# The last four gate tiles of a recurrent stage made as two wide seven-product pairs

## The chip, the cores and the metric

The kernel runs on one core of one Trainium2 chip. The metric is the time of one execution on the device in microseconds (us), as the median of several runs. The core's engines are TensorE (PE, matmuls), VectorE (DVE), ScalarE (ACT), GpSimd (POOL) and SyncE (SP); here POOL and SP mostly issue DMAs, SP the weights.

## The reference

One decoder layer on 512 tokens of width 1024, all in float32: a SwiGLU product, a gated merge of attention and a linear recurrence, and a second SwiGLU product, each with norms around it. The part at hand is the merge:

```python
proj = u @ w_in[l]
q, k, v, xr, yr, gl = jnp.split(proj, splits, axis=-1)
...
attn_d = attn.astype(x.dtype).reshape(B, S, ATTN_OUT_WIDTH) @ w_attn_branch[l]
rec = rg_lru_branch(xr, conv_w[l], conv_b[l], lru_w_x[l], lru_b_x[l],
                    lru_w_a[l], lru_b_a[l], lru_a_param[l]) * jax.nn.gelu(yr)
rec_d = rec @ w_rec_branch[l]
gates = jax.nn.sigmoid(gl).reshape(B, S, N_BRANCHES, D_MODEL)
merged = gates[:, :, 0] * attn_d + gates[:, :, 1] * rec_d
h = h + rms_norm(merged @ w_out[l], mix_norm_post[l])
```

`rg_lru_branch` is a causal convolution over four tokens (`xr` to `xc`), two gates of `xc` (sigmoids of products with block-diagonal weights, four heads of 256), and the scan h = a·h + b along the tokens.

## The kernel before, in words

Activations lie transposed: 128 of the 1024 features on the partitions, the 512 tokens along the row. So a result of width 1024 is eight tiles of 128x512, and a product over 1024 features has eight chunks of 128.

*Three-product form.* PE multiplies in the format fp32r, and the kernel keeps float32's accuracy by splitting each operand in a high and a low part (`split`, L303 and L304: ACT writes the high part, DVE subtracts it for the low part). `mm3` adds high·high, high·low and low·high (L316 to L318). A plain tile is 8 chunks x 3 = 24 matmuls of 128x512. Its weights (128x1024) come by one DMA on SP's queue into one of four raw buffers and go through one split into one of four buffers `w8`.

*Seven-product form.* Two neighbouring tiles and the two halves of the tokens make a 2x2 product by blocks, which Strassen's scheme (in Winograd's form) does in seven products instead of eight. The sums of the input (`um_t` for the plain halves and the "forms" p4 to p7) are made once, ahead of the stage. The sums of the weights are made for each pair by `w_forms_within`: two raw buffers, four additions of 512 (L725 to L729), and splits of 512, 1024, 1024 and 1024. `seven_wide` then issues the products, each as 4 matmuls of 512 (L791) and 4 of 256 (L794); between them ACT moves a partial sum from one accumulator to the next (L799, `move`), and `fold` (L805 on ACT, L807 or L809 on DVE) and `sum_of` (L815, L817, L819) bring the two halves of a bank together.

*The stage.* `LRU_ORDER` lists the steps: the branch that goes through gelu (`branch`, four pairs already in seven-product form), the convolution input (`conv`, plain tiles with taps at L1610), the recurrence's gates and scan (`gates`, `gates_of` and `recur`: L1669 to L1698), and the gate gl's second half for the merge (`gate1`: plain tiles, copied by L1651 to `sig`, sigmoid at L1644). Before, gate tiles 0 and 1 follow conv 2, tiles 2, 3, 4 follow conv 3, and tiles 5, 6, 7 follow gates 3. Behind the loop come the products with w_rec: tiles 0 to 2 at once (chunks 0 to 5, then 6, then 7), then tiles 3 to 7; L1741 multiplies each by the gate, L1742 adds the gated attention output (`facc`), L304 splits the sum.

Each engine runs its instructions in one fixed order. The framework's scheduler sets it when the program is built: by the order of the code, priorities (`tc.high_priority`) that put a weight split or an evacuation ahead by so many steps, and the buffers of each pool. `prepare` makes the weights of the next step's pair while the present one runs.

*Buffers.* `um_t` and forms lie in the pools with the tags `b` (16 KB parts, named big) and `rb`. Before, the second half of `rec` (the recurrence's output, chunks 4 to 7) takes the place of an `rb` form after branch 3, and the residual h is read back from DRAM (`kept_m`) into `b` at the same place (L1709).

Of the kernel before, what the change touches and what calls it, by code (L numbers as in the profile page):

```python
# [10 lines left out]
F32 = mybir.dt.float32  # L11
F32R = mybir.dt.float32r
# [4 lines left out]
P = 128  # L17
T = 512
D = 1024
KC = D // P  # L20
# [21 lines left out]
WARM = 10  # L42
QKB = 6
CB = 6
GATE1 = ((), (0, 1), (2, 3, 4), (5, 6, 7))

LRU_ORDER = (("branch", 0), ("branch", 1), ("conv", 0), ("branch", 2), ("gates", 0), ("conv", 1), ("branch", 3),
             ("gates", 1), ("conv", 2), ("gate1", 1), ("gates", 2), ("conv", 3), ("gate1", 2), ("gates", 3),
             ("gate1", 3))

PAIRED = tuple(("branch", h) for h in range(4))
COLUMN = {"conv": 36, "branch": 44, "gate1": 60}

# [127 lines left out]
def hybrid_layer(ctx: ExitStack, tc: tile.TileContext, xT: bass.AP, xN: bass.AP, wst: bass.AP,  # L185
                 first: bass.AP, rows: bass.AP, consts: bass.AP, bias: bass.AP, out: bass.AP):
    nc = tc.nc
    DVE, ACT, PE = nc.vector, nc.scalar, nc.tensor

    cpool = ctx.enter_context(tc.tile_pool(name="cpool", bufs=1))  # L190
# [5 lines left out]
    dpool = ctx.enter_context(tc.tile_pool(name="dpool", bufs=1, space=bass.MemoryType.DRAM))  # L196
# [3 lines left out]
    cst = cpool.tile([P, CONST_W], F32, name="cst")  # L200
    ones = cpool.tile([P, P], F32, name="ones")
    eps = cpool.tile([P, 1], F32, name="eps")
    facc = cpool.tile([P, KC, T], F32, name="facc")
    hs = {}

    def new_h():
        hs["t"] = [bpool.tile([P, 4, T], F32, name="h", tag="b") for _ in range(2)]
# [5 lines left out]
    def hb(b, sl=slice(0, D)):  # L213

        return hs["t"][b // 2].rearrange("p k t -> p (k t)")[:, b % 2 * D:b % 2 * D + D][:, sl]
# [86 lines left out]
    def split(dh, dl, src):  # L302
        state["split"] = ACT.activation(dh, src, AF.Copy).ins  # L303
        state["low"] = DVE.tensor_sub(dl, src, dh.bitcast(F32)).ins  # L304
# [48 lines left out]
    HALVES = (slice(0, HB), slice(HB, T))  # L353
# [422 lines left out]
    def seven_wide(t, w, g, u, seen=lambda ap: ap, then=lambda: None, sign=1.0):  # L776


        b, z, y, v, o = (acc_ps() for _ in range(5))

        def two(ps):
            return ps[:, :HB], ps[:, HB:]

        def product(p, ps, start):
            at = t[p].at
            part, cross = ps, two(ps)[1]
            if len(at(BOTH, 0).shape) == 3:
                part = ps.rearrange("q (s c) -> q s c", s=2)
            ks = [slice(k * P, (k + 1) * P) for k in range(4)]
            for k in range(4):  # L790
                PE.matmul(part, w[p][:, 0, ks[k]], at(BOTH, k), start=start and k == 0, stop=False,  # L791
                          skip_group_check=True)
            for k in range(4):
                last = PE.matmul(cross, w[p][:, 1, ks[k]], at(0, k), start=False, stop=k == 3, skip_group_check=True)  # L794
            state["product"] = last.ins

        def move(dst, src):
            with tc.high_priority(offset=EVAC):
                return ACT.activation(dst, src, AF.Copy).ins  # L799

        def fold(ps, dst=None, sign=1.0):
            out = tpool.tile([P, HB], F32, name="c", tag="c", bufs=CB) if dst is None else dst
            x, y_ = two(ps) if dst is None else map(seen, two(ps))
            with tc.high_priority(offset=EVAC):
                ACT.activation(out, x, AF.Copy, scale=sign)  # L805
                if sign > 0:
                    DVE.tensor_add(out, y_, out)  # L807
                else:
                    DVE.scalar_tensor_tensor(out, y_, sign, out, op0=ALU.mult, op1=ALU.add)  # L809
            return out  # L810

        def sum_of(dst, ps, c, sign=1.0):
            x, y_ = two(ps)
            with tc.high_priority(offset=EVAC):
                DVE.tensor_add(c, x, c)  # L815
                if sign > 0:
                    DVE.tensor_add(dst, seen(y_), seen(c))  # L817
                else:
                    DVE.scalar_tensor_tensor(dst, y_, sign, c, op0=ALU.mult, op1=ALU.subtract)  # L819

        product("p1", b, True)
        move(y, b)
        product("p5", z, True)
        c5 = fold(z)
        product("p6", y, False)
        move(v, y)
        c6 = fold(y)
        product("p2", b, False)
        fold(b, g[0])
        product("p7", v, False)  # L830
        moved = move(o, v)
        sum_of(u[1], v, c5, sign)
        with tc.issue_after(moved):
            then()
        product("p3", z, False)
        sum_of(g[1], z, c6)
        product("p4", o, False)
        fold(o, u[0], sign)
# [350 lines left out]
    for b in range(4):  # L1189
# [2 lines left out]
    um_t = [big([P, 2, 2, T]) for _ in range(4)]  # L1192
    um = Act(*([um_t[k // 2][:, s, k % 2, :] for k in range(KC)] for s in range(2)))
    kept_m = dpool.tile([4, P, D], F32, name="kept_m")
    bd1 = Boundary(0.5, grow2, lambda i: [(slice(2 * j, 2 * j + 2), um_t[2 * i + j][:, 0], um_t[2 * i + j][:, 1])
                                          for j in range(2)], kept_m)

# [10 lines left out]
    kpool = kpool_cm.__enter__()  # L1208

    def rec_half():  # L1210

        return kpool.tile([P, 8, T], F32R, name="rb", tag="rb")
# [29 lines left out]
    with ExitStack() as mx:  # L1242
# [38 lines left out]
        def values_two(steps, then):  # L1281
# [78 lines left out]
            for j in range(2):  # L1360
# [4 lines left out]
        t, steps = forms_of(lambda i, j: Form(lambda s, k: um_t[2 * i + k // 2][:, s, k % 2, HALVES[j]]),  # L1365
                            apool, False, rec_half)
# [175 lines left out]
        for c in range(KC):  # L1542
            ps = acc_ps()
            if c % 2 == 0:
                two = fetch(("attn", c))
            gemm(ps, [w[:, c % 2 * 512:c % 2 * 512 + 512] for w in two], attn)
            DVE.tensor_mul(facc[:, c, :], ps, facc[:, c, :])

    with ExitStack() as mx:
        rpool = mx.enter_context(tc.tile_pool(name="rec", bufs=1))  # L1550
        rec_t = rpool.tile([P, 8, T], F32R, name="rec")
        rec = Act([rec_t[:, i, :] for i in range(4)], [rec_t[:, 4 + i, :] for i in range(4)])
        rec.n = KC
        sig = rpool.tile([P, KC, T], F32, name="sig")
        paired = {}
# [90 lines left out]
        def gate1(hd):  # L1646
            for c in GATE1[hd]:
# [3 lines left out]
                    DVE.tensor_copy(sig[:, c, :], ps)  # L1651
                late.append(c)

        def gates_of(hd, then):
            wh, wl = fetch(("lru", hd))
            then()
            a_ = wh.rearrange("p (w i c) -> p w i c", w=2, i=2)
            b_ = wl.rearrange("p (w i c) -> p w i c", w=2, i=2)
            gs = {}
            sigmoids()  # L1660
            for w, bn in ((1, "ba"), (0, "bx")):
                for j in range(2):
                    ps = aux_ps() if w or not j else acc_ps()
                    for i in range(2):
                        js = slice(j * P, (j + 1) * P)
                        mm3(ps, a_[:, w, i, js], b_[:, w, i, js], rec.hi[2 * hd + i], rec.lo[2 * hd + i],
                            i == 0, i == 1)
                    g = lpool.tile([P, T], F32, name="gt", tag="gt", bufs=6)
                    ACT.activation(g, ps, AF.Sigmoid, bias=col(bn, 2 * hd + j))  # L1669
                    gs[w, j] = g  # L1670
            return [gs[1, j] for j in range(2)], [gs[0, j] for j in range(2)]
# [27 lines left out]
                split(rec.hi[c], rec.lo[c], ge)  # L1699

        for i, (what, hd) in enumerate(LRU_ORDER):
            if i and LRU_ORDER[i - 1] == PAIRED[-1]:

                rec_t = rec_half()
                rec.hi += [rec_t[:, c, :] for c in range(4)]
                rec.lo += [rec_t[:, 4 + c, :] for c in range(4)]
                new_h()
                for b in range(4):
                    nc.gpsimd.dma_start(hb(b), kept_m[b])  # L1709

            def then():
                if i + 1 < len(LRU_ORDER):
                    prepare(LRU_ORDER[i + 1])

            if what == "gates":
                recur(hd, gels.pop(hd), *gates_of(hd, then))
                continue
            if what == "conv":
                conv(hd, then)
                continue  # L1720
            then()
            {"branch": branch, "gate1": gate1}[what](hd)
            if what == "branch" and hd % 2:
                gelus((hd - 1, hd))
        sigmoids()
        state["ahead"] = AHEAD
        lpool_cm.__exit__(None, None, None)

        mg = act_big("mg")

# [4 lines left out]
        for c in range(KC):  # L1735
            if c < 3:
                ps = pss[c]
            else:
                ps = acc_ps()
                gemm(ps, fetch(("rec", c)), rec)  # L1740
            DVE.tensor_mul(sig[:, c, :], ps, sig[:, c, :])  # L1741
            DVE.tensor_add(sig[:, c, :], sig[:, c, :], facc[:, c, :])  # L1742
            split(mg.hi[c], mg.lo[c], sig[:, c, :])

    kpool_cm.__exit__(None, None, None)

# [156 lines left out]
```

## Time and profile before

| | before |
|---|---|
| median of 3 runs | 1206.55 us (1206.17 to 1207.76) |
| the profiled execution | 1205.68 us, of it 1203.9 us span |
| granted TensorE clock | 0.999 |
| PE / DVE / ACT busy | 1196.1 / 1039.3 / 839.5 us |

The recurrent stage lies between about 620 and 815 us of the span. A timeline row gives start, duration, engine, line, operation, what is written and read, and in brackets the idle time before it with what ended that. Names such as `w` and `raw` are buffers of a tag; the shape is partitions x elements. Windows give busy time and count for PE, weight load, DVE, ACT and POOL, then the granted clock, the share of the DMA engines and GB/s.

### The profile page before, as it was taken

The numbers are of one execution on the slowest core, as the hardware profiler recorded it, in microseconds if no ns is written. First come the engines' busy times: TensorE is split into PE (matmuls) and PEld (weight loads), VectorE is DVE, ScalarE is ACT, GpSimd is POOL, SyncE is SP. The second block draws the span as 40 slices with busy tenths as digits, with TensorE's granted clock in tenths as the row PEclk, the third lists the DMA queues.
The fourth block names the chain that finished last, engine by engine and source line by source line (L and its number), as shares of the span: only waits on it lengthen the run. The fifth ranks groups of instructions, "written<-read, shape, count | busy, mean of one in ns | idle before, by whom it ended". The sixth has DMA issues, their size and how long they took to land.

```text
span 1203.9 us, 18693 instructions
## 1 busy us (share of the span) xinstructions
PE 1196.1 (99%) x7138; PEld 1064.4 (88%) x7138; DVE 1039.3 (86%) x1641; ACT 839.5 (70%) x1455; POOL 26.1 (2%) x51
## 2 busy tenths in 40 slices
PE   9999999999999999999999999999999999999997
PEld 8899999999888889888888888888899999898996
DVE  7999888989689999999878899874898888889974
ACT  7566787887566676777846988734566687878763
POOL 0000000000011000000000000000100000000000
PEclk9999999999999999999999999999999999999999
DMA  7234343334725232222323533235443333333441
GB/s 268 88 97 139 117 140 108 139 112 153 251 98 165 71 97 89 96 88 79 110 73 116 172 116 97 85 109 190 143 140 106 123 122 124 123 125 121 140 175 71
DMA packets 45818, 149.76 MB, mean 124 GB/s; under 512 B 5152, under 2 KB 8608, under 8 KB 45728
## 3 DMA queue, kind: packets, MB, share of 16 engines
q1 hardware_dynamic: 38160, 131.09, 33.2%
q0 software_dynamic: 7280, 17.30, 4.3%
q8 instruction: 56, 0.92, 0.3%
q14 instruction: 34, 0.28, 0.1%
q10 hardware_dynamic: 288, 0.17, 0.0%
HBM read 138.06 MB, written 6.29 MB: 120 GB/s over the span
## 4 chain that ended last, share of the span: by engine, by line
PE 97%; DVE 1%; ACT 1%; DMA 0%; issue 0%; DVEq 0%
PE acc L791 12%; PE acc L741 9%; PE acc L743 9%; PE acc L742 9%; PE acc L318 7%; PE acc L316 7%; PE acc L317 7%; PE acc L794 6%; PE aux L1076 4%; PE aux L1077 4%; PE aux L1078 4%; PE acc L434 2%; PE acc L433 2%; PE acc L432 2%; PE aux L434 1%; PE aux L433 1%
## 5 line engine op out<-in xcount | busy, mean ns | idle before, releaser
L304 DVE TENSOR_TENSOR w<-raw,w 128x1024 fp32r<-128x1024 f32 (+1 forms) x272 | 296.9, 1099 | 34.1 <-ACT w L303 32.9
L303 ACT ACTIVATE w<-raw 128x1024 fp32r<-128x1024 f32 (+1 forms) x272 | 259.1, 958 | 87.6 <-PE acc L318 45.9
L741 PE MATMUL acc<-big,w 128*128 128x256 f32 x788 | 223.0, 283 | 0.2 <-ACT acc L755 0.2
L743 PE MATMUL acc<-big,w 128*128 128x256 f32 x788 | 223.0, 283 | 0.0
L742 PE MATMUL acc<-big,w 128*128 128x256 f32 x788 | 223.0, 283 | 0.0
L741 PEld LDWEIGHTS acc<-big,w 128*128 128x128 f32 x788 | 151.0, 192 | 1.6 <-ACT acc L755 0.4
L742 PEld LDWEIGHTS acc<-big,w 128*128 128x128 f32 x788 | 151.0, 192 | 1.3
L743 PEld LDWEIGHTS acc<-big,w 128*128 128x128 f32 x788 | 151.0, 192 | 0.0
L791 PE MATMUL acc<-big,w 128*128 128x512 f32 x452 | 124.5, 395 | 0.0
L1076 PE MATMUL aux<-w,xf 128*128 128x512 f32 x224 | 87.5, 391 | 0.0
L1077 PE MATMUL aux<-w,xf 128*128 128x512 f32 x224 | 87.5, 391 | 0.0
L1078 PE MATMUL aux<-w,xf 128*128 128x512 f32 x224 | 87.1, 389 | 0.0
L791 PEld LDWEIGHTS acc<-big,w 128*128 128x128 f32 x452 | 77.4, 188 | 10.1
L794 PEld LDWEIGHTS acc<-big,w 128*128 128x128 f32 x452 | 69.2, 188 | 9.3
L794 PE MATMUL acc<-big,w 128*128 128x256 f32 x452 | 73.1, 282 | 0.0
L304 DVE TENSOR_TENSOR w<-s,w 128x1024 fp32r<-128x1024 f32 x51 | 62.3, 1221 | 2.1 <-ACT w L303 1.8
L303 ACT ACTIVATE w<-s 128x1024 fp32r<-128x1024 f32 x51 | 53.8, 1055 | 7.9 <-PE acc L743 4.9
L316 PE MATMUL acc<-xf,w 128*128 128x512 f32 (+1 forms) x168 | 58.8, 352 | 0.0
L317 PE MATMUL acc<-xf,w 128*128 128x512 f32 (+1 forms) x168 | 58.6, 349 | 0.0
L318 PE MATMUL acc<-xf,w 128*128 128x512 f32 (+1 forms) x168 | 58.6, 349 | 0.0
L1078 PEld LDWEIGHTS aux<-w,xf 128*128 128x128 f32 x224 | 42.1, 188 | 9.0
L316 PE MATMUL acc<-big,w 128*128 128x512 f32 x128 | 49.9, 390 | 0.0
(464 smaller groups left out, 2876.4 us busy)
## 6 DMA issues: line engine op xcount, KB each, us to landing
raw<-in_w SPq DMA_DIRECT2D x232, 512.0 KB, 3.5
big<-xf POOLq DMA_DIRECT2D x6, 512.0 KB, 3.3
gains<-in_rows POOLq DMA_DIRECT2D x5, 512.0 KB, 6.2
h<-in_x SPq DMA_DIRECT2D x8, 256.0 KB, 5.3
h<-in_xn POOLq DMA_DIRECT2D x4, 512.0 KB, 6.3
kept_m<-h POOLq DMA_DIRECT2D x4, 512.0 KB, 2.9
vals<-in_w SPq DMA_DIRECT2D x4, 512.0 KB, 6.2
h<-kept_m POOLq DMA_DIRECT2D x4, 512.0 KB, 6.0
```

What stands on the lines that cost most here:

```text
L303: state["split"] = ACT.activation(dh, src, AF.Copy).ins
L304: state["low"] = DVE.tensor_sub(dl, src, dh.bitcast(F32)).ins
L316: PE.matmul(ps, wh, xh, start=first, stop=False)
L317: PE.matmul(ps, wh, xl, start=False, stop=False)
L318: PE.matmul(ps, wl, xh, start=False, stop=last)
L741: PE.matmul(ps, wh, xh, start=start and k == 0, stop=False, skip_group_check=True)
L742: PE.matmul(ps, wh, xl, start=False, stop=False, skip_group_check=True)
L743: state["product"] = PE.matmul(ps, wl, xh, start=False, stop=k == 3, skip_group_check=True).ins
L791: PE.matmul(part, w[p][:, 0, ks[k]], at(BOTH, k), start=start and k == 0, stop=False, skip_group_check=True)
L794: last = PE.matmul(cross, w[p][:, 1, ks[k]], at(0, k), start=False, stop=k == 3, skip_group_check=True)
L1076: PE.matmul(ps, xh, wh, start=first and j == 0, stop=False, skip_group_check=True)
L1078: PE.matmul(ps, xl, wh, start=False, stop=j == 1, skip_group_check=True)
```

## The change

Gate tiles 4 to 7 are made in two pairs in wide seven-product form ("gate2", heads 2 and 3), both after gates 3; gate1 keeps tiles 0 to 3. The input forms are now needed until the stage's end, so the place that `rec`'s second half took from them must come from elsewhere: it is laid over `facc` (as `recu`), whose content, attention's gated output, is written to DRAM (`kept_a`) two tiles at a time as it is made. After the stage's loop it is read back into a buffer `rb` (`attn_o`), and h is read back there too, no longer after branch 3. Lines from L200 on move by one and more: L304 is L305, L316 to L318 are L317 to L319, L791 is L792, L1610 is L1615, L1685 is L1696, L1689 is L1700, L1697 is L1708, L1741 is L1749, L1742 is L1750.

```diff
-GATE1 = ((), (0, 1), (2, 3, 4), (5, 6, 7))
+GATE1 = ((), (0, 1), (2, 3), ())
...
-             ("gate1", 3))
+             ("gate2", 2), ("gate2", 3))
...
-PAIRED = tuple(("branch", h) for h in range(4))
-COLUMN = {"conv": 36, "branch": 44, "gate1": 60}
+PAIRED = tuple(("branch", h) for h in range(4)) + (("gate2", 2), ("gate2", 3))
+COLUMN = {"conv": 36, "branch": 44, "gate1": 60, "gate2": 60}
...
-    facc = cpool.tile([P, KC, T], F32, name="facc")
+    fpool = ctx.enter_context(tc.tile_pool(name="fpool", bufs=1))
+    facc = fpool.tile([P, KC, T], F32, name="facc", tag="facc")
...
+    kept_a = dpool.tile([4, P, D], F32, name="kept_a")
...
             DVE.tensor_mul(facc[:, c, :], ps, facc[:, c, :])
+            if c % 2:
+                nc.gpsimd.dma_start(kept_a[c // 2], facc[:, c - 1:c + 1, :].rearrange("p k t -> p (k t)"))
...
-        rec = Act([rec_t[:, i, :] for i in range(4)], [rec_t[:, 4 + i, :] for i in range(4)])
+        rec_u = fpool.tile([P, 8, T], F32R, name="recu", tag="facc")
+        rec = Act(*([x[:, o + i, :] for x in (rec_t, rec_u) for i in range(4)] for o in (0, 4)))
...
+        def gate2(hd):
+            w = paired.pop(("gate2", hd))
+            tiles = (2 * hd, 2 * hd + 1)
+            seven_wide(t, w, *([sig[:, c, h] for h in HALVES] for c in tiles), sign=-1.0)
+            late.extend(tiles)
...
-            if i and LRU_ORDER[i - 1] == PAIRED[-1]:
-
-                rec_t = rec_half()
-                rec.hi += [rec_t[:, c, :] for c in range(4)]
-                rec.lo += [rec_t[:, 4 + c, :] for c in range(4)]
-                new_h()
-                for b in range(4):
-                    nc.gpsimd.dma_start(hb(b), kept_m[b])
-
...
         sigmoids()
         state["ahead"] = AHEAD
         lpool_cm.__exit__(None, None, None)
+        attn_o = kpool.tile([P, KC, T], F32, name="rb", tag="rb")
+        for i in range(4):
+            nc.gpsimd.dma_start(attn_o[:, 2 * i:2 * i + 2, :].rearrange("p k t -> p (k t)"), kept_a[i])
+        new_h()
+        for b in range(4):
+            nc.gpsimd.dma_start(hb(b), kept_m[b])
...
-            DVE.tensor_add(sig[:, c, :], sig[:, c, :], facc[:, c, :])
+            DVE.tensor_add(sig[:, c, :], sig[:, c, :], attn_o[:, c, :])
             split(mg.hi[c], mg.lo[c], sig[:, c, :])
+        facc = fpool.tile([P, KC, T], F32, name="facc", tag="facc")
```

How the order of instructions changes is shown at three places. In the names, `w_` with a number is one split weight buffer, `raw` a loaded weight, `gt`, `th`, `r_` the recurrence's gate, scan and factor, `ge` the recurrence's output, `c` a folded half. First DVE before, from the multiplication that ends head 2 (L1698, its second tile) to the first rows of head 3 (L1685):

```order
L304 TENSOR_TENSOR w_7782<-raw,w_7782 128x1024
L304 TENSOR_TENSOR rb<-ge,rb 128x512
L1698 TENSOR_TENSOR ge<-th,ge 128x512
L304 TENSOR_TENSOR rb<-ge,rb 128x512
L1689 TENSOR_TENSOR gt<-gt,sig 128x512 x2
L1685 TENSOR_SCALAR gt<-th,r_7685 128x512
L1686 TENSOR_SCALAR r_7685<-gt,r_7685 128x512
L304 TENSOR_TENSOR w_7820<-raw,w_7820 128x1024
```

Between the last split of head 2's output and head 3's L1685 stand only the two L1689 rows. DVE after, from the same split on (`recu` in place of `rb`):

```order
L305 TENSOR_TENSOR recu<-ge,recu 128x512
L730 TENSOR_TENSOR raw<-raw 128x512
L305 TENSOR_TENSOR w_7621<-raw,w_7621 128x1024
L808 TENSOR_TENSOR sig<-acc,sig 128x256
L726 TENSOR_TENSOR raw<-raw 128x512
L305 TENSOR_TENSOR w_7622<-raw,w_7622 128x1024
L808 TENSOR_TENSOR c<-acc,c 128x256
L305 TENSOR_TENSOR w_7712<-raw,w_7712 128x1024
L727 TENSOR_TENSOR raw<-raw 128x512
L1700 TENSOR_TENSOR gt<-gt,sig 128x512
L808 TENSOR_TENSOR c<-acc,c 128x256
L728 TENSOR_TENSOR raw<-raw 128x512
```

Seven more rows follow (L816 twice, L818, L820, L810, the split of w_7713 and an L730) before head 3's first L1696, which was L1685: 18 rows in all, with the weights of both pairs among the folds of the first. The end of DVE's part in the stage, after:

```order
L1709 TENSOR_TENSOR ge<-th,ge 128x512
L1708 TENSOR_SCALAR th<-gt 128x512
L305 TENSOR_TENSOR w_7915<-raw,w_7915 128x1024
L1709 TENSOR_TENSOR ge<-th,ge 128x512
L305 TENSOR_TENSOR recu<-ge,recu 128x512
L305 TENSOR_TENSOR w_7910<-raw,w_7910 128x1024
L305 TENSOR_TENSOR recu<-ge,recu 128x512
L305 TENSOR_TENSOR w_8008<-raw,w_8008 128x1024
L1749 TENSOR_TENSOR sig<-acc,sig 128x512 x2
```

w_7905, w_7910 and w_7915 are the weights of tiles 0, 1 and 2 of the product with w_rec; the splits of the last two now stand among the last rows of head 3's recurrence. Where PE, after, comes to them:

```order
L319 MATMUL acc<-recu,w_7905 128x512
L317 MATMUL acc<-rec,w_7910 128x512
L318 MATMUL acc<-rec,w_7910 128x512
L317 MATMUL acc<-rec,w_7915 128x512
L318 MATMUL acc<-rec,w_7915 128x512
L317 MATMUL acc<-rec,w_8008 128x512
L318 MATMUL acc<-rec,w_8008 128x512
L319 MATMUL acc<-rec,w_7915 128x512
```

PE begins tiles 1, 2 and 3 (w_8008) with their high parts, then does tile 2, and behind that tile 1 from its first low part on; before, it took tiles 0, 1 and 2 one after the other. On POOL's queue `kept_a<-facc` x4 comes new, then stand `h<-kept_m` x4 and `rb<-kept_a` x4, in this order, both behind the last pair.

More of the change, by code (lines that the diff above doesn't have):

```diff
@@ L1721, in hybrid_layer @@
             then()
-            {"branch": branch, "gate1": gate1}[what](hd)
+            {"branch": branch, "gate1": gate1, "gate2": gate2}[what](hd)
             if what == "branch" and hd % 2:
```

## Prediction

> **What bounds the kernel.** I read the page's busy times and its chain first, then busy times by stretch, then the timelines of TensorE and VectorE where the edit sits.
>
> ```profile
> span 1203.9 us, 18693 instructions
> PE 1196.1 (99%) x7138; PEld 1064.4 (88%) x7138; DVE 1039.3 (86%) x1641; ACT 839.5 (70%) x1455; POOL 26.1 (2%) x51
> ...
> PE 97%; DVE 1%; ACT 1%; DMA 0%; issue 0%; DVEq 0%
> ```
>
> TensorE (PE) is busy for 99% of the span, and 97% of the chain that ended last is its own work. A microsecond of matmul taken away is won only where the engines that feed it keep up. So the question is how VectorE (DVE, 86% over the whole) stands in this stage.
>
> ```profile
> 618.00:733.90 115.90, 115.90 (x588) 98.51 (x587) 98.64 (x143) 91.84 (x130) 2.16 (x4) 1.00 0.36 119
> 733.90:780.70 46.80, 46.80 (x207) 38.58 (x206) 43.51 (x58) 36.83 (x49) 0.00 (x0) 1.00 0.28 90
> 780.70:815.00 34.30, 34.30 (x151) 28.14 (x151) 21.66 (x29) 11.74 (x15) 0.00 (x0) 1.00 0.36 123
> ```
>
> After the window's length come the busy times of PE, weight load, DVE, ACT, POOL, and then the granted clock. PE is full in all three. In the 46.80 us that hold gate tiles 2 to 7 and recurrences 2 and 3, DVE is busy for 43.51: it has 3.3 us to spare. Behind 780.70, in the product with w_rec, it has 12.6.
>
> ```profile
> 733.96 0.75 DVE L1610 SCALAR_TENSOR_TENSOR sig<-xr,first,sig 128x512 f32<-128x512 f32 x1
> ...
> 758.12 0.69 DVE L304 TENSOR_TENSOR rb<-ge,rb 128x512 fp32r<-128x512 f32 x1 [0.70 <-ACT rb L303]
> ...
> 762.45 0.69 DVE L1685 SCALAR_TENSOR_TENSOR gt<-th,r 128x512 f32<-128x512 f32 x1 [2.43 <-ACT r L1684]
> ...
> 779.97 0.71 DVE L304 TENSOR_TENSOR rb<-ge,rb 128x512 fp32r<-128x512 f32 x1
> ...
> 814.82 0.69 DVE L1741 TENSOR_TENSOR sig<-acc,sig 128x512 f32<-128x512 f32 x1 [2.34 <-PE acc L318]
> ```
> ```profile
> 785.09 0.39 PE L316 MATMUL acc<-rb,w 128*128 128x512 f32 x1
> ...
> 787.15 0.39 PE L316 MATMUL acc<-rec,w 128*128 128x512 f32 x1
> ...
> 792.64 0.39 PE L316 MATMUL acc<-rec,w 128*128 128x512 f32 x1
> ```
>
> The spare time is two waits, 0.70 and 2.43 us. The last split of the recurrence's output (779.97) ends at 780.68; PE reads that chunk first at 785.09. So DVE leads by 4.4 us at the end of the stretch. Only then does PE run alone to the stage's end at 814.82. A product tile there is 792.64 − 787.15 = 5.49 us for 24 matmuls, 0.2288 each.
>
> **The change, part by part.** *TensorE.* The wide pair is there already, in branches 0 and 1:
>
> ```profile
> 621.64 1.09 PE L791 MATMUL acc<-big,w 128*128 128x512 f32 x4
> ...
> 641.17 0.39 PE L316 MATMUL acc<-big,w 128*128 128x512 f32 x1
> ...
> 754.28 0.40 PE L316 MATMUL acc<-big,w 128*128 128x512 f32 x1
> ...
> 770.65 0.40 PE L316 MATMUL acc<-rec,w 128*128 128x512 f32 x1
> ```
>
> Two pairs run from 621.64 to 641.17: 9.77 us each. Gate tiles 5, 6 and 7 run from 754.28 to 770.65: 5.46 each, 10.91 for two. PE saves 1.15 a pair, **−2.3 us**.
>
> *VectorE.* Its rows overlap a little, so their price is the distance from one start to the next:
>
> ```profile
> 630.61 0.41 DVE L819 SCALAR_TENSOR_TENSOR ge<-acc,c 128x256 f32<-128x256 f32 x1
> 630.94 0.42 DVE L817 TENSOR_TENSOR ge<-acc,c 128x256 f32<-128x256 f32 x1
> ...
> 746.66 0.68 DVE L1651 COPY sig<-acc 128x512 f32<-128x512 f32 x1
> 747.26 0.68 DVE L1695 SCALAR_TENSOR_TENSOR th<-th,r 128x512 f32<-128x512 f32 x1
> 747.86 1.22 DVE L304 TENSOR_TENSOR w<-raw,w 128x1024 fp32r<-128x1024 f32 x1
> 749.00 0.69 DVE L1696 TENSOR_TENSOR gt<-gt,th 128x512 f32<-128x512 f32 x1
> ```
>
> So 0.33 to 0.335 us for a row of 256, 0.60 to 0.605 for one of 512, 1.135 to 1.14 for one of 1024. A pair makes its weights with 4 additions of 512 (L725 to L729), one split of 512 and three of 1024, and folds its sums with 8 rows of 256 (L807 to L819): 5 × 0.605 + 3 × 1.135 + 8 × 0.335 = 9.1 us. Two plain tiles need two splits of 1024 and two copies (L1651): 3.5. Two pairs therefore add 11.3 us to DVE while they take 2.3 from PE.
>
> How much of it lies ahead of the point where PE is let go? By the changed order I count DVE's rows from the L1610 that starts at 733.96 up to the split of the weights for tile 1 of the w_rec product (w_7910, the third fence on the change): 79 rows. Against the 58 of before, which end with the last recurrence split, they hold 16 more of 256, 5 more of 512 (8 additions and 2 narrow splits come; 4 copies and the last recurrence split, which now stands behind w_7910, go) and one more of 1024: 16 × 0.335 + 5 × 0.605 + 1.135 = 9.5 us. Before had 780.68 − 733.96 = 46.7, of which 43.5 is busy; so now 53.0 us of work, until 787.0 if DVE never waits.
>
> Will it wait? The 2.43 us before L1685 is DVE ahead of PE and ACT: the gates of head 3 had to come through them, and behind the recurrence split DVE had only the two L1689 rows. Now 18 rows, all but one of the pairs, stand between that split and that L1685: 5 × 0.605 (an L1689 among them) + 4 × 1.135 + 8 × 0.335 = 10.2 us of work. Walking the new order on all engines with these durations, each row starting when its engine and its inputs are there, I find 0.8 us of waiting left, and DVE through at 787.2 to 787.8; I take the average of that walk and the count, **787.4**. The ends are no wait, 787.0, and the whole 3.2 us of before, 790.2.
>
> Behind w_7910's split PE has 157 matmuls left in its order: 16 of tile 1, 5 of tile 2, 18 for the last two chunks of tiles 0 to 2, 22 of tile 3 and 96 of tiles 4 to 7. At 0.2288 they take 35.9 us. The last product ends at 787.4 + 35.9 = 823.3, and its multiply starts 0.2 later, at 823.5, against 814.82: **+8.7 us** (ends +8.3 and +11.5). This includes PE's saving: PE must stand for about 8.7 + 2.3 = 11 us between 744 and 788, in pieces of 0.2 to 2.3 us before the pair's products whose weights are late. Behind 815 the rows follow in the same order, so the shift goes to the end.
>
> *ScalarE.* Per pair it gains three splits of 1024, one of 512, three moves and four folds and loses two splits.
>
> ```profile
> L799 ACT ACTIVATE acc<-acc 128x512 f32<-128x512 f32 x6 | 3.5, 583 | 1.8 <-PE acc L794 1.7
> L805 ACT ACTIVATE c<-acc 128x256 f32<-128x256 f32 x4 | 1.5, 377 | 0.8 <-PE acc L794 0.8
> ```
>
> At most 3 × 0.58 + 4 × 0.38 + 1.05 + 0.63 = 4.9 us more a pair; 36.8 + 9.9 = 46.7 of now 53 us. It has room, so it costs nothing beyond the late halves inside DVE's walk; if that fails, up to the 2 us of one move late behind sigmoids.
>
> *Transfers.* POOL's queue gains 4 spills of attention's output and 4 loads of it, and its 4 loads of h, made at 681.7 before, move behind the last pair; SP's weight loads keep their order.
>
> ```profile
> raw<-in_w SPq DMA_DIRECT2D x232, 512.0 KB, 3.5
> ...
> kept_m<-h POOLq DMA_DIRECT2D x4, 512.0 KB, 2.9
> ...
> h<-kept_m POOLq DMA_DIRECT2D x4, 512.0 KB, 6.0
> ```
>
> The spills have 2.9 us to land and over 100 us until facc's place is written as recu: nothing. The eight loads start between about 767 and 778; the first addition that reads attention's output comes at about 799, 21 us later, against 6.0 us to land. Cost zero; without that cover DVE's L1742 row would hold the splits queued behind it, some 6 us. The weights of the w_rec product land amid these loads, at 3.5 us alone and 6.0 if they fare like h, with about 8 to spare.
>
> *Sum.* On the profiled execution: 1205.68 + 8.7 = 1214.4. The median of the runs, 1206.55, lies 0.87 above it; so **1215.2 us**.
>
> **Clock.** PE will stand often; does it lose its clock?
>
> ```profile
> 1197.00:1202.00 5.00, 0.60 (x6) 0.40 (x4) 2.72 (x11) 0.77 (x3) 0.00 (x0) 1.00 0.55 206
> 1202.00:1203.00 1.00, 0.00 (x0) 0.00 (x0) 0.00 (x0) 0.00 (x0) 0.00 (x0) 0.78 0.02 5
> 1203.00:1203.90 0.90, 0.00 (x0) 0.00 (x0) 0.00 (x0) 0.00 (x0) 0.00 (x0) 0.50 0.00 0
> ```
>
> At the kernel's end PE stops 0.60 us into the first window and is still granted 1.00 for 4.4 us; then it falls to 0.50. My gaps are at most 2.3 us, with work between. The Trainium skill, "TensorE: Matmul & The Clock Gate", Part 1 (The HAM clock gate), says that after one idle window of about 3.4 us the clock is halved until it has been busy for as long again. The trace agrees with the half, and its 4.4 us fits a window that had to begin first; no gap in this trace shows a fall amid work. As a mechanism of this kernel: where several gaps join into one of 4 us, a stretch of some 4 us at 0.50 loses 2 us, two of them 4.
>
> **Rivals.** *Faster: the pairs are covered.* The saving of 2.3 us stands, 1204.3. For it: branches 0 and 1 run as such pairs with PE full. Against it: it needs the added 9.5 us within 3.2 idle + 4.4 lead = 7.6, and the weight splits must not queue behind recurrence rows; the order puts them there. It decides where DVE is through before PE wants tile 1's weights, at about 770. I give 0.04, half of it for no change.
>
> *Milder: only the overflow counts.* If what is late is merely the last recurrence split, at 788, PE has the 9 rows of chunk 7 and 118 of tiles 3 to 7 behind it: 788 + 127 × 0.2288 + 0.2 = 817.3, +2.4, 1209.0. Against it: w_7910 stands ahead of that split and is needed 30 matmuls sooner. 0.08.
>
> *Worse.* DVE waits as before (+11.5), a weight lands 6 us late behind the eight loads, or the clock falls (+2 to +4 on top): 1217.5 to 1221. For it: ACT runs sigmoids between the pair's moves, and one table more is loaded. 0.16.
>
> *Main.* +7 to +10.5, 0.72.
>
> **The numbers.** Leaving out the gain and most of the far ends, the range runs from 1210.5 to 1219.5. 0.2% (2.4 us) is about what a measurement of this kernel tells from no change: faster 0.02, same 0.03, slower 0.95.
>
> **What would show it.** PE busy in the stretch from 734 to 815 unchanged less 2.3, with some 11 us of idle put down to DVE and ACT w of L305 and to L800; DVE without a pause above 1 us from 734 to 787; the last L1749 near 823.5; granted clock 1.00; landings of h and rb ended before 790. I am wrong if PE's idle there is under 5 us (DVE had slack that its start-to-start distances hide), or if DVE itself waits for raw or for rb (transfers).

## The result

| | before | after |
|---|---|---|
| median of runs | 1206.02 us (6 runs, 1205.35 to 1207.76) | 1215.49 us (6 runs, 1214.98 to 1216.69) |
| the profiled execution | 1205.68 us, span 1203.9 | 1215.66 us, span 1213.8 |
| time of the last w_rec product's multiply in the span | 814.82 | 825.12 |

The changed kernel is slower by 9.5 us: ratio 1.0078, 95% interval 1.0065 to 1.0091. The forecast was 1215.2 us. Page of the changed kernel: span, busy times, chain.

```profile
span 1213.8 us, 18791 instructions
...
PE 1199.1 (99%) x7154; PEld 1065.2 (88%) x7154; DVE 1050.2 (87%) x1665; ACT 847.8 (70%) x1474; POOL 30.4 (3%) x59
...
PE 90%; DVE 7%; ACT 2%; issue 1%; DMA 0%; DVEq 0%; ACTq 0%
```

DVE has 11 us more work, and for the first time it carries a share of the chain (7%, 1% before). PE's busy time has not fallen by 2.3 us but risen by 3: a matmul's row lasts 0.39 us where the next one starts 0.23 later, so the tail of the last one ahead of each wait counts as busy, and rows at a low clock are longer. The windows of the changed kernel, columns as in the prediction:

```profile
733.90:780.70 46.80, 41.26 (x192) 32.49 (x191) 46.01 (x72) 41.60 (x64) 2.92 (x6) 0.96 0.32 113
780.70:789.00 8.30, 6.86 (x29) 5.07 (x28) 8.30 (x10) 5.35 (x7) 1.33 (x3) 1.00 0.85 314
789.00:815.00 26.00, 26.00 (x114) 21.25 (x114) 17.38 (x24) 8.89 (x11) 0.00 (x0) 1.00 0.44 143
```

PE idles for 5.5 + 1.4 us where it was full before; DVE, busy for 43.5 of 46.8 before, is busy for 46.0 and then for all of 8.3. Behind 789 PE is full again. DVE's timeline, after:

```profile
735.09 0.75 DVE L1615 SCALAR_TENSOR_TENSOR sig<-xr,first,sig 128x512 f32<-128x512 f32 x1
...
768.29 0.42 DVE L810 SCALAR_TENSOR_TENSOR sig<-acc,sig 128x256 f32<-128x256 f32 x1 [0.33 <-ACT sig L806]
...
777.30 0.69 DVE L1706 SCALAR_TENSOR_TENSOR th<-th,r 128x512 f32<-128x512 f32 x1 [0.33 <-ACT th L1702]
...
787.45 1.24 DVE L305 TENSOR_TENSOR w<-raw,w 128x1024 fp32r<-128x1024 f32 x1
...
825.12 0.69 DVE L1749 TENSOR_TENSOR sig<-acc,sig 128x512 f32<-128x512 f32 x1 [2.37 <-PE acc L319]
```

From the first L1615 to the end of w_7910's split (787.45 + 1.24 = 788.69) are 53.6 us with 0.7 us of waiting. The L1615 starts 1.1 us later than its partner of before (733.96); that shift is there ahead of all that the change slows (the stage's first pair starts at 622.80 for 621.64), and since the multiply is 10.3 us later here but the medians differ by 9.5, most of it is a difference between two executions. PE in the same stretch, after (matmuls of the pairs are L792 and L795):

```profile
751.80 0.74 PE L795 MATMUL acc<-big,w 128*128 128x256 f32 x4 [0.49 <-DVE w L305]
754.71 2.07 PE L792 MATMUL acc<-big,w 128*128 128x512 f32 x4 [2.17 <-ACT acc L800]
756.58 1.05 PE L795 MATMUL acc<-big,w 128*128 128x256 f32 x4
757.94 1.19 PE L792 MATMUL acc<-big,w 128*128 128x512 f32 x4 [0.30 <-ACT w L304]
759.87 0.74 PE L795 MATMUL acc<-big,w 128*128 128x256 f32 x4 [0.74 <-DVE w L305]
...
786.02 0.50 PE L319 MATMUL acc<-rec,w 128*128 128x512 f32 x1 [1.44 <-DVE w L305]
...
788.74 0.50 PE L319 MATMUL acc<-rec,w 128*128 128x512 f32 x1
```

The waits lie where the prediction put them: inside the pairs, the first above all, and at the weights of w_rec's tiles; the longest is for a move of ScalarE (L800). The row at 788.74 is the first that needs w_7910's low part, ended 0.05 us before; from it to the last multiply are 36.4 us with no further stop. The rows at 754.71 and 756.58 take 2.9 us for eight matmuls that took 1.4 at 621.64 before: the granted clock had fallen, as windows of one microsecond of the changed kernel show (first column PE's busy time, clock before the last two).

```profile
753.00:754.00 1.00, 0.00 (x0) 0.00 (x0) 1.00 (x2) 1.00 (x2) 0.00 (x0) 1.00 0.00 0
754.00:755.00 1.00, 0.29 (x1) 0.29 (x2) 1.00 (x2) 0.66 (x2) 0.00 (x0) 0.59 0.00 0
755.00:756.00 1.00, 1.00 (x3) 0.81 (x3) 1.00 (x2) 0.00 (x0) 0.00 (x0) 0.50 0.00 0
756.00:757.00 1.00, 1.00 (x4) 0.81 (x4) 1.00 (x3) 0.69 (x2) 0.00 (x0) 0.50 0.00 0
757.00:758.00 1.00, 0.70 (x4) 0.40 (x3) 1.00 (x3) 1.00 (x2) 0.00 (x0) 0.70 0.00 0
```

Counted by starts, PE loses some 11.4 us between 730 and 800: 6.8 in waits of its timeline, 1.5 to the clock, the rest in the matmuls next to the waits (the one ahead runs out, the first behind takes 0.50 us for 0.39).

### The profile page after: what moved, and what is told of

The parts are those of the page before. It is cut to its first block, busy times and chain, and to the rows that moved or that the text cites. A ratio compares the mean times of both kernels' runs of the same rounds, so it can differ in the third digit from the quotient of the medians.

```text
span 1213.8 us, 18791 instructions
## 1 busy us (share of the span) xinstructions
PE 1199.1 (99%) x7154; PEld 1065.2 (88%) x7154; DVE 1050.2 (87%) x1665; ACT 847.8 (70%) x1474; POOL 30.4 (3%) x59
## 4 chain that ended last, share of the span: by engine, by line
PE 90%; DVE 7%; ACT 2%; issue 1%; DMA 0%; DVEq 0%; ACTq 0%
PE acc L792 12%; PE acc L742 9%; PE acc L744 9%; PE acc L743 9%; PE acc L795 6%; PE acc L319 5%; PE acc L317 5%; PE acc L318 5%; PE aux L1077 4%; PE aux L1078 4%; PE aux L1079 4%; PE acc L433 2%; PE acc L435 2%; PE acc L434 2%; DVE w L305 1%; PE aux L435 1%
## 5 line engine op out<-in xcount | busy, mean ns | idle before, releaser
L305 DVE TENSOR_TENSOR w<-raw,w 128x1024 fp32r<-128x1024 f32 (+1 forms) x276 | 300.7, 1097 | 33.9 <-ACT w L304 32.8
L304 ACT ACTIVATE w<-raw 128x1024 fp32r<-128x1024 f32 (+1 forms) x276 | 261.9, 956 | 91.3 <-PE acc L319 49.0
L742 PEld LDWEIGHTS acc<-big,w 128*128 128x128 f32 x788 | 151.0, 192 | 1.4
L743 PEld LDWEIGHTS acc<-big,w 128*128 128x128 f32 x788 | 151.0, 192 | 1.3
L744 PEld LDWEIGHTS acc<-big,w 128*128 128x128 f32 x788 | 151.0, 192 | 0.0
L792 PE MATMUL acc<-big,w 128*128 128x512 f32 x492 | 137.3, 398 | 3.5 <-ACT acc L800 3.0
L792 PEld LDWEIGHTS acc<-big,w 128*128 128x128 f32 x492 | 84.8, 189 | 15.8 <-ACT acc L800 3.7
L795 PEld LDWEIGHTS acc<-big,w 128*128 128x128 f32 x492 | 75.5, 189 | 12.1 <-DVE w L305 2.1
L795 PE MATMUL acc<-big,w 128*128 128x256 f32 x492 | 80.1, 283 | 1.2 <-DVE w L305 1.2
L305 DVE TENSOR_TENSOR w<-s,w 128x1024 fp32r<-128x1024 f32 x51 | 62.2, 1219 | 2.0 <-ACT w L304 1.8
L304 ACT ACTIVATE w<-s 128x1024 fp32r<-128x1024 f32 x51 | 53.8, 1055 | 7.8 <-PE acc L744 4.9
L317 PE MATMUL acc<-xf,w 128*128 128x512 f32 (+1 forms) x168 | 59.2, 354 | 0.0
L318 PE MATMUL acc<-xf,w 128*128 128x512 f32 (+1 forms) x168 | 58.7, 350 | 0.0
L319 PE MATMUL acc<-xf,w 128*128 128x512 f32 (+1 forms) x168 | 58.5, 349 | 0.0
L800 ACT ACTIVATE acc<-acc 128x512 f32<-128x512 f32 x72 | 42.3, 588 | 10.1 <-PE acc L795 8.1
```

The lines of the kernel that those rows point to most:

```text
L317: PE.matmul(ps, wh, xh, start=first, stop=False)
L318: PE.matmul(ps, wh, xl, start=False, stop=False)
L742: PE.matmul(ps, wh, xh, start=start and k == 0, stop=False, skip_group_check=True)
L743: PE.matmul(ps, wh, xl, start=False, stop=False, skip_group_check=True)
L744: state["product"] = PE.matmul(ps, wl, xh, start=False, stop=k == 3, skip_group_check=True).ins
```

## Experiments

Theory A, the prediction's: the amount of work in VectorE's queue up to w_7910's split is the cost. Rivals: transfers; ScalarE's moves and the clock; the place of the pairs. All differences are of medians, against the runs of before on the same chip.

**The buffers alone.** The spill, the place of rec's second half and the reloads, with the tiles plain:

```diff
-GATE1 = ((), (0, 1), (2, 3), ())
+GATE1 = ((), (0, 1), (2, 3, 4), (5, 6, 7))
...
-             ("gate2", 2), ("gate2", 3))
+             ("gate1", 3))
```

> Only the buffer part of the change: attention's output goes to DRAM and back, rec's second half lies over facc, h is read back late; gate tiles 2 to 7 are plain as before. Theory (VectorE's added work is the whole cost): no difference from before, -0.5 to +0.8 us. Rival (transfers: four writes and eight loads meet the weights): +1.5 to +6 us, with waits of VectorE or ScalarE for raw or rb.

Measured: 1205.82 against 1206.03, ratio 0.9998 (0.9989 to 1.0007). The spills and the other places cost nothing. One thing it does not test: with no pair left the reload of attention's output starts at 689.6 already, not at 780. In the changed kernel these loads show no harm either:

```profile
kept_a<-facc POOLq DMA_DIRECT2D x4, 512.0 KB, 3.0
...
h<-kept_m POOLq DMA_DIRECT2D x4, 512.0 KB, 5.4
rb<-kept_a POOLq DMA_DIRECT2D x4, 512.0 KB, 5.3
```

The last rb load is issued at 781.5 and the first addition that reads it starts at 801.3; no wait of DVE there is put down to a transfer.

**Less of it: one pair, no sums, narrow pairs.** Three kernels take 4 to 6 us from DVE's 11.3.

```diff
-GATE1 = ((), (0, 1), (2, 3), ())
+GATE1 = ((), (0, 1), (2, 3), (6, 7))
...
-             ("gate2", 2), ("gate2", 3))
+             ("gate2", 2), ("gate1", 3))
```

> Half the change: tiles 4 and 5 as a wide pair behind gates 3, tiles 6 and 7 plain behind it. Theory (VectorE's queue is the bound, once 3.2 us of idle and 4.4 us of lead are used up): 4.75 us of added work fit in, so TensorE keeps its 1.15 us: -1.2 to +0.8 us against before. Rival (each pair stops TensorE by its own waits: moves on ScalarE, late forms, the clock): half of the whole, +3.5 to +5.5 us.

```diff
+            summed = key[1] < COLUMN["gate2"]
...
-            DVE.tensor_add(u1, u0, u1)
-            DVE.tensor_add(u0, u0, g0)
-            DVE.tensor_add(g0, u1, g0)
+            if summed:
+                DVE.tensor_add(u1, u0, u1)
+                DVE.tensor_add(u0, u0, g0)
+                DVE.tensor_add(g0, u1, g0)
...
-            DVE.tensor_add(g1, g0, g1)
+            if summed:
+                DVE.tensor_add(g1, g0, g1)
```

> The change with the eight weight additions of the two gate pairs left out on VectorE (the gate tiles 4 to 7 are then not the reference's); all else, ScalarE's work and the order included, as it is. Theory (VectorE's amount of work): 8 x 0.605 = 4.8 us less, so +4.6 us against before (+3.8 to +5.4). Rival (ScalarE's moves behind sigmoids, and the clock that fell to 0.50 for some 3 us): hardly less than the whole change, +7.5 to +9.5.

```diff
-            seven_wide(t, w, *([sig[:, c, h] for h in HALVES] for c in tiles), sign=-1.0)
+            two_tiles(w, *(sig[:, c, :] for c in tiles))
```

> The change with the two gate pairs in the narrow seven-product form that branch 3 has (products of 256 columns, 10.04 us of TensorE a pair by branch 3's rows for 9.77; two rows of 256 on VectorE a pair for eight). Theory (VectorE's amount): 12 x 0.335 = 4.0 us less on VectorE, so +5.4 us against before (+4.5 to +6.3), though TensorE has 0.5 us more to do. Rival (TensorE's own count, or the weight forms' lateness alone): +8.5 to +10.

Measured: +7.7 us (ratio 1.0062, 1.0047 to 1.0077), +7.8 (1.0064, 1.0047 to 1.0081) and +7.3 (1.0062, 1.0047 to 1.0077). All three miss theory A's numbers, the one-pair kernel most clearly: half the added work costs four fifths of the whole. Its rows, PE's, ScalarE's and then DVE's, and its window of 750 to 763 (DVE's busy time is third):

```profile
755.27 2.07 PE L792 MATMUL acc<-big,w 128*128 128x512 f32 x4 [4.08 <-ACT acc L800]
...
763.90 1.65 PE L792 MATMUL acc<-big,w 128*128 128x512 f32 x6 [1.39 <-DVE c L808]
```
```profile
751.76 0.63 ACT L304 ACTIVATE recu<-ge 128x512 fp32r<-128x512 f32 x1 [1.76 <-DVE ge L1709]
...
754.62 0.60 ACT L800 ACTIVATE acc<-acc 128x512 f32<-128x512 f32 x1
```
```profile
784.01 0.68 DVE L305 TENSOR_TENSOR recu<-ge,recu 128x512 fp32r<-128x512 f32 x1
794.54 1.37 DVE L1749 TENSOR_TENSOR sig<-acc,sig 128x512 f32<-128x512 f32 x2 [9.85 <-PE acc L319]
```
```profile
750.00:763.00 13.00, 8.43 (x32) 6.86 (x30) 13.00 (x18) 10.31 (x16) 1.07 (x2) 0.74 0.18 46
```

DVE is through at 784.7 and then idles for 9.85 us: its amount bounds nothing at the end. Nearly all of the loss lies between 749 and 764, in the pair itself: 4.1 us waiting for a move on ScalarE, some 3 us at a granted clock of 0.50 (from about 754.6 to 761.4), 1.4 at a fold. The move stands behind a split of head 2's output, and ScalarE had waited 1.76 us for DVE to come to that. And there, for 13 us, DVE has no gap, though it had 3.1 us of idle in the same window before. In the kernel without sums the rebuilt order put two w_rec splits behind the whole recurrence, and PE waited 3.2 us for the first; so the 4.8 us were not taken away where they counted, and since its granted clock stayed at 1.00, its +7.8 owes nothing to the clock. In the kernel with narrow pairs PE waits 1.2, 1.2, 1.8 and 1.4 us between 750 and 760, for DVE and for ScalarE in turn. New theory B: a second limit stands just below the first. A wide pair asks DVE and ScalarE for sums, splits, moves and folds at short notice, and directly behind gates 3 both still hold head 2's recurrence.

**Dose behind the pair and ahead of it.** One line of the recurrence is repeated, 8 rows of 512 on DVE (4.8 us) for one head:

```diff
-                DVE.tensor_mul(ga, th, r0)
+                for _ in range(5 if hd == 3 else 1):
+                    DVE.tensor_mul(ga, th, r0)
```

> The change with eight rows of 512 more on VectorE in head 3's recurrence (each of two products computed five times; the same result): 4.8 us more work. Amount theory, in its simple form: +4.8 on top of the change, +14 against before. Theory by place: the rebuilt order puts the splits of the weights of w_rec's tiles 1 and 2 ahead of head 3's last rows, so TensorE waits for the last recurrence split alone, with 127 matmuls behind it and not 157: the last split ends at about 794, +7 to +10 against before.

> The one-pair kernel with the same eight more rows on VectorE. Its trace shows VectorE through at 784.7 and then idle for 9.85 us, so VectorE's amount bounds nothing there: the 4.8 us are hidden, +7.0 to +8.2 against before, as without them. Rival (VectorE's amount is what the one pair pays as well): +12.

With `hd == 2` in its place, so ahead of the pair:

> The one-pair kernel (+7.5 to +8) with the eight more rows of 512 on VectorE in head 2's recurrence, ahead of the pair, where in head 3's they cost +0.9. Theory (the pair's weight sums and splits queue on VectorE behind head 2's recurrence, and VectorE has no gap from 734 to 763 there): nearly all of the 4.8 us is paid, +11 to +13 against before. Rival (the pair loses its time to moves behind ScalarE's sigmoids, whatever VectorE has queued): +7.5 to +9.

> The kernel before with the same eight rows more in head 2's recurrence: control. Theory: its 3.2 us of idle and 4.4 us of lead take up most of the 4.8 us (a plain tile asks for nothing of VectorE but a split made well ahead), +1 to +2.5 us. Rival (VectorE's queue is so full that each added row is paid here too): +4 to +5.

| kernel | without | with 4.8 us in head 3 | with 4.8 us in head 2 |
|---|---|---|---|
| before | 0 | | +2.3 (1.0019, 1.0010 to 1.0028) |
| one pair | +7.7 | +8.6 (1.0072, 1.0058 to 1.0086) | +15.0 (1.0123, 1.0108 to 1.0139) |
| both pairs | +9.5 | +14.4 (1.0119, 1.0105 to 1.0133) | |

With both pairs 4.8 us of DVE work cost 4.9 us, as the simple form of theory A says and not my refinement: PE did not wait for the last recurrence split but 3.7 us for weights of w_rec, and behind them no more:

```profile
785.53 0.80 PE L319 MATMUL acc<-rec,w 128*128 128x512 f32 x1 [3.67 <-DVE w L305]
```

That the two numbers are so near is in part luck: that gap took the granted clock to 0.50 until 788.5, which cost some 1.5 us of the 4.9. With one pair the same rows cost 0.9 behind the pair, which the intervals do not tell from nothing, and 7.3 ahead of it, more than their own length, since PE's longer waits also kept the clock at 0.50 until about 771:

```profile
754.81 1.22 PE L795 MATMUL acc<-big,w 128*128 128x256 f32 x4 [4.11 <-DVE w L305]
756.70 2.08 PE L792 MATMUL acc<-big,w 128*128 128x512 f32 x4 [0.67 <-ACT acc L800]
...
761.62 2.08 PE L792 MATMUL acc<-big,w 128*128 128x512 f32 x4 [2.00 <-ACT w L304]
...
766.60 1.65 PE L792 MATMUL acc<-rb,w 128*128 128x512 f32 x3 [2.05 <-ACT w L304]
```

The kernel before takes half of them for nothing: its slack is real, but not all of it is where it is needed. PE there waits 0.9 us for a weight split and 0.8 for the last recurrence split, while DVE still idles for 3.0 us ahead of head 3's L1685.

**Less work ahead, in the whole change.** The taps of head 3's convolution are left out:

```diff
-                    for t in (2, 1, 0):
+                    for t in (2, 1, 0) if hd < 3 else ():
```

> The whole change (+9.4) with the taps of head 3's convolution left out on VectorE, six rows of 0.66 us ahead of the pairs (the recurrence of head 3 then gets other values). Theory (VectorE's queue from 734 to the last weight split): 4.0 us less, so +5 to +6.3 against before. Rival (waits on ScalarE and the clock carry it): +8.5 to +9.5.

Measured: +7.6 us (1.0064, 1.0050 to 1.0077): 1.9 us won of 4.0, less than theory A says and more than its rival. PE's rows show other waits taking over:

```profile
752.05 0.74 PE L795 MATMUL acc<-big,w 128*128 128x256 f32 x4 [1.45 <-DVE w L305]
756.01 3.26 PE L792 MATMUL acc<-big,w 128*128 128x512 f32 x7 [3.21 <-ACT w L304]
```

DVE now has idle moments (0.6, 1.0 and 0.6 us between 760 and 770, on ScalarE), because the three engines wait for each other in turn. With this, four ways of taking work away end between +7.3 and +7.8, each by other waits; that one common limit stands behind them is not shown.

**Plain tiles first.** The one-pair kernel with plain tiles 4 and 5 behind gates 3, then the pair:

```diff
-GATE1 = ((), (0, 1), (2, 3), ())
+GATE1 = ((), (0, 1), (2, 3), (4, 5))
...
-             ("gate2", 2), ("gate2", 3))
+             ("gate1", 3), ("gate2", 3))
...
-            then()
+            last = what == "gate1" and LRU_ORDER[i - 1] == ("gates", 3)
+            if not last:
+                then()
             {"branch": branch, "gate1": gate1, "gate2": gate2}[what](hd)
+            if last:
+                then()
```

> The one-pair kernel with the order turned: behind gates 3 first the plain tiles 4 and 5, then the pair of 6 and 7. VectorE, ScalarE and TensorE have the same work as in the one-pair kernel (+7.5). New theory (the pair lost its time because it stood directly behind gates 3, with head 2's recurrence and head 3's sigmoids ahead of its forms, moves and folds): 11 us later they are through, so -1.2 to +1.5 us against before. Rival (a pair in this stretch costs its waits wherever it stands): +5 to +8.

Measured: +5.1 us (1.0039, 1.0027 to 1.0052), at the low end of the rival's range. Theory B in the form "11 us later they are through" is wrong; the wait has only another recurrence ahead of it. Still, the place is worth 2.6 us of the 7.7. PE's row, then ScalarE's:

```profile
767.75 1.52 PE L792 MATMUL acc<-rb,w 128*128 128x512 f32 x4 [2.77 <-ACT acc L800]
```
```profile
761.35 0.63 ACT L304 ACTIVATE recu<-ge 128x512 fp32r<-128x512 f32 x1 [1.96 <-DVE ge L1709]
761.89 0.71 ACT L1691 ACTIVATE th<-gt,po 128x512 f32<-128x512 f32 x1
762.60 1.28 ACT L1693 ACT_TABLE_LOAD   x1
763.90 1.34 ACT L1693 ACTIVATE r<-gt,sp 128x512 f32<-128x512 f32 x2
765.14 1.13 ACT L1695 ACTIVATE r<-r 128x512 f32<-128x512 f32 x2
766.18 1.04 ACT L304 ACTIVATE w<-raw 128x1024 fp32r<-128x1024 f32 x1
767.13 0.57 ACT L800 ACTIVATE acc<-acc 128x512 f32<-128x512 f32 x1
```

The move that PE needs at about 765 stands in ScalarE's queue behind a split that waited 1.96 us for DVE, and then behind the start of head 3's recurrence.

**Pairs early in the stage.** One kernel has tiles 0 to 3 in two pairs behind branch 1 and gates 0:

```diff
-GATE1 = ((), (0, 1), (2, 3, 4), (5, 6, 7))
+GATE1 = ((), (), (4,), (5, 6, 7))
...
-LRU_ORDER = (("branch", 0), ("branch", 1), ("conv", 0), ("branch", 2), ("gates", 0), ("conv", 1), ("branch", 3),
-             ("gates", 1), ("conv", 2), ("gate1", 1), ("gates", 2), ("conv", 3), ("gate1", 2), ("gates", 3),
+LRU_ORDER = (("branch", 0), ("branch", 1), ("gate2", 0), ("conv", 0), ("branch", 2), ("gates", 0), ("gate2", 1),
+             ("conv", 1), ("branch", 3), ("gates", 1), ("conv", 2), ("gates", 2), ("conv", 3), ("gate1", 2),
+             ("gates", 3), ("gate1", 3))
```

> From the kernel before: gate tiles 0 to 3 as two wide pairs early in the stage (behind branch 1 and behind gates 0, ahead of branch 3, so that the forms' place is given up as before and nothing goes to DRAM), tiles 4 plain behind conv 3, 5 to 7 plain behind gates 3 as before. New theory (a pair stops TensorE where VectorE and ScalarE are still working off a recurrence; the runs with one pair and with less VectorE work cost +7.4 to +7.8 all the same): early, where VectorE had over 10 us of idle time in 40, the pairs run covered and TensorE's 2.3 us are won, -2.6 to -1.0 us against before. Rival (a gate pair costs its 11 us of VectorE wherever it stands, since the recurrences need them): +2 to +9.

Measured: +14.5 us. This kernel computes something else: the buffer `sig` holds the convolution's output until the recurrence has read it, so early gate values and the convolution overwrite each other, and their steps are ordered by that. It says nothing on the place of the pairs. So one pair was put early with the gate values in the spilled facc's place:

```diff
-GATE1 = ((), (0, 1), (2, 3), ())
+GATE1 = ((), (2, 3), (4, 5), (6, 7))
...
+LRU_ORDER = (('branch', 0), ('branch', 1), ('gate2', 0), ('conv', 0), ('branch', 2), ('gates', 0), ('conv', 1), ('branch', 3), ('gates', 1), ('conv', 2), ('gate1', 1), ('gates', 2), ('conv', 3), ('gate1', 2), ('gates', 3), ('gate1', 3))
...
-        rec_u = fpool.tile([P, 8, T], F32R, name="recu", tag="facc")
+        gate = fpool.tile([P, KC, T], F32, name="gate", tag="facc")
```

> One gate pair (tiles 0 and 1) put where VectorE has room, behind branch 1; gate values lie over the spilled facc, rec's second half over the forms as before; the plain tiles 2 to 7 are then left as covers by twos (before conv 2's gates, before conv 3's and behind gates 3). Theory: the pair itself runs without a stop of TensorE (-1.15), but behind gates 3 only two plain tiles stand over head 3's recurrence, 5.5 us less cover than before against 4.4 us of lead, and VectorE's 5.7 us more come on top: TensorE waits for the last recurrence splits, +2 to +4 us against before. Rival (place alone decides; early it is free): -1.5 to -0.5.

Measured: +4.5 us (1.0037, 1.0025 to 1.0050), a little above the +2 to +4 expected. The three pairs now run from 622.28 to 651.6 without a wait, so an early pair does win its 1.15 us; it is lost at the end, where head 3's last recurrence splits come late behind two plain tiles instead of three:

```profile
784.92 0.50 PE L315 MATMUL acc<-rb,w 128*128 128x512 f32 x1 [1.52 <-ACT rb L302]
...
787.09 0.50 PE L316 MATMUL acc<-rb,w 128*128 128x512 f32 x1 [1.67 <-DVE rb L303]
```

None of these versions beats the kernel before.

## Why the prediction was right, and where it was not

- *TensorE's saving* of 1.15 us a pair: the early pairs, which wait for nothing, run at the 9.77 us assumed. Right.
- *VectorE's ledger*: 53.4 us from the first L1610 to w_7910's split were forecast, with 0.8 of waiting; it took 53.6 with 0.7. Right: the rows themselves show that this queue sets the end. The added 4.8 us that cost 4.9, some 1.5 of it by the clock, agree but weigh less.
- *157 matmuls behind it*: 36.1 us forecast to the multiply, 36.4 measured. The last wait of any length is at w_7915's split, one before w_7910's (1.44 us at 786.02); the first row that needs w_7910's starts 0.1 us behind its turn, so both splits let PE go at nearly the same time. The last multiply, forecast 8.7 us later, came 9.2 later than a start of the stretch that is common to both.
- *Transfers at nothing*: right, by the kernel with the buffers alone for the spills and by the landings for the loads.
- *ScalarE "costs nothing beyond the late halves"*: right for the sum, as DVE hid it, but wrong as a view of the engine. PE's longest wait in the stretch, 2.17 us, is for one of its moves, and in the one-pair kernel one held PE for 4.1 us, twice the 2 us that I put down for a late move.
- *The clock*: the step that failed. I held gaps of 2.3 us too short to lose it. It fell to 0.50 within a gap of 2.17 us. Its 1.5 us are hidden here, since DVE waited for 0.7 us in all and was later still; the one-pair kernel pays some 3 us for it.
- *The faster rival's conditions*: I named two, that the added work stays within 7.6 us of idle time and lead, and that no weight split queues behind recurrence rows. For the one-pair kernel I counted on the first alone. Its added work was about half of the 9.5 us, and it still lost 7.7. Slack of a stretch is no pool: DVE had 5.3 us of it behind 777, where one pair could not use it, and 3.1 between 750 and 763, where some 6.5 us of sums and splits were asked for at once.
- *Slips that do not reach the sum*: before had 57 rows and not 58 (the window's count takes in the end of the split from 732.81); the 18 rows ahead of head 3's first L1696 hold six of 512 and not five, 10.8 us.

So the time was right for the mechanism that is the limit, but I did not see that other waits, nearly as costly, stood behind it. How ScalarE's queue, DVE's lateness and the clock share the +7.3 to +7.8 was not separated: each run that changed one moved the others. The kernel that would take ScalarE's move alone out of the queue was not run.

## What to carry to other kernels

Fewer matmuls win nothing where TensorE is fed by engines without room: count what the new form adds to each feeding queue up to the row that TensorE waits for, and then count the matmuls behind that row. Slack must be counted where it is asked for, since idle time 20 us later is no cover for work that is needed now. A plain product asks only for weights made well ahead, whereas this seven-product form asks other engines for an answer between its products. For one pair, the place directly behind a long elementwise chain was the worst of the three that were run (+7.7, against +5.1 and +4.5). When a cause has been confirmed, halve it: if half of it costs nearly as much, something else is behind it.

## What the runs showed of the hardware

The clock fell sooner than the end of the kernel before suggested: there PE's last matmul ends at 1197.6 and the fall comes 5.0 us later, at 1202.6 (my 4.4 ended with the window). In the changed kernel it was 1.00 until 754 and 0.59 over the next microsecond, so it fell some 1.6 us into a gap of 2.17 us that followed another of 0.49, and it came back after some 3.4 us. In the kernel with one early pair two gaps of 1.5 and 1.7 us, 0.5 us of work apart, were enough for a granted clock of 0.93 over 777 to 790; it fell at 788.2, over 1 us after PE had gone on. The Trainium skill, "TensorE: Matmul & The Clock Gate", Part 1 (The HAM clock gate), names an idle window of about 3.4 us as what halves the clock; these gaps are shorter, and in the 3.4 us before the fall PE had been busy for 1.3, so a whole window without work was not needed. The return after some 3.4 us agrees with what that section says of the busy window.

It was not the length of one gap that decided. In the kernel without sums PE stood for 3.16 us and the clock stayed at 1.00. The traces record when the granted clock changes: amid the work it is low for 3.41 us at a time or for a multiple of that, 6.82 with one pair and 17.07 with one pair and more work ahead. The 3.41 us that end in a fall have PE busy for at most 1.67 us; those that begin and end at 1.00 have 1.74 (without sums, over its gap) and more, but for one of 1.66 near the end of the early-pair kernel. So the limit seems to be near half of such a step, which no run tested by itself.
